# A two-layer decoder trunk in one kernel: MLP products in runs of one width, convolution tiles behind the next chunk's whole projection

## The chip, the cores and the metric

The kernel runs on one core of a Trainium2 chip. It uses that core's engines: PE (matmul), DVE (vector), ACT (activation), POOL, and SP, which here only issues DMAs. The metric is the time of the whole program on the device in microseconds, as the median of several runs.

## The reference, cut to what matters

Input is `x`, 512 tokens of 1024 channels, and a memory of 256 tokens. There are two layers. Layer 0 mixes tokens with a gated recurrence and pooling, layer 1 with a convolution module. Each layer then has a cross-attention into the memory and a gated MLP. The change touches the convolution module and the MLP:

```python
def conformer_conv(x, norm, w1, b1, dw_w, dw_b, ln_g, ln_b, w2, b2):
    h = rms_norm(x, norm) @ w1 + b1
    h = jax.nn.glu(h, axis=-1)
    h = causal_dwconv(h, dw_w, dw_b)
    h = jax.nn.silu(layer_norm(h, ln_g, ln_b))
    return h @ w2 + b2

def conv_ffn(x, norm, w_up, dw_w, dw_b, w_down):
    h = rms_norm(x, norm) @ w_up
    g = causal_dwconv(h[..., :D_FF], dw_w, dw_b)
    u = h[..., D_FF:]
    return (jax.nn.gelu(g) * u) @ w_down

for layer in range(DEPTH):
    ...
    x = x + cross_attn(x, mem, xa_norm[layer], xa_mem_norm[layer], xa_wq[layer], ...)
    x = x + conv_ffn(x, f_norm[layer], f_w_up[layer], f_dw_w[layer], ...)
return rms_norm(x, final_norm)
```

The convolution of the module has 31 taps per channel, `D_FF` is 3072.

## The kernel before

Channels lie on the 128 partitions and the 512 tokens along a row, so an activation is 8 chunks of 128 x 512. Every float32 operand of a large matmul is split into a high and a low part: ACT rounds the high part (a copy to the type fp32r), and DVE or POOL subtracts it from the operand (`split`, line 622). A full product then takes three matmuls, high x high, high x low and low x high (`mm3`, line 629).

**Who sets the order.** The program is written down first and ordered afterwards. Each call on an engine becomes a node of a recorder (`Recorder`, line 201) with a duration from `cost` (line 271). `plan` (line 319) plays the nodes through on a model of the engines. PE takes them nearly in the order of the code (a window of 60 nodes), the others by due time. Calls inside `rec.atomic()` are one node and are not torn apart. The order that comes out is fixed for each engine, and so is each tile's buffer. All planned instructions are issued in one line, 498, so the profile shows L498 for nearly everything and the tiles tell operations apart: `mm` and `aux` are PSUM accumulators (5 and 2 of them), `stat` one for statistics, `wf` raw weights, `wr` split weights (18 slots for both), `act` and `actf` activations, `h` the gated product in the conformer and the padded gate branch in the MLP, `tmp` short-lived.

**The MLP** (`ffn`, line 978) has 24 chunks of up-projection in each layer, in 6 groups of 4, and after each group's ups the previous group's down-projection, woven in. An up chunk (`up`, line 1006) is a 2 x 2 block scheme with seven products in place of eight (`product`, line 1012). Each product multiplies four row blocks. `b` holds the high parts of 256 columns and the low parts of the same 256 side by side, so one matmul of the high weights with all 512 columns and one of the low weights with the 256 high ones make a product of the block. From chunk 3 on (`PLAIN`, `both` in the code) the 512-wide form is used: for each j, first the 512-wide one, then the 256-wide one. In the first three chunks of a layer all matmuls have 256 columns. `copy` (line 1023) takes the running accumulator `x` to SBUF three times on the way.

**The conformer** (`conformer`, line 1331) has for each of its 8 chunks two projections of 24 matmuls with 512 columns. The first, the gate, goes through ACT's sigmoid (`gate`, line 1336). The second is multiplied with it by DVE (`gated`, line 1348), and four DMAs on SP then stack the result: each takes 32 channels and lays them out four times, shifted by one token each (`window(4)`). The convolution is shared. PE does 8 of the 31 taps with 32-wide tiles on the stacked copies into an `aux` accumulator (`conv_pe`, line 1370, two groups of four tiles; the last chunk has eight groups and so all its taps on PE). POOL and ACT do 4 taps (N_POOL), DVE does the other 19 by adding into the same accumulator (`conv`, line 1387). DVE's `merge` (line 1407) puts both together and so frees the accumulator; after chunk 3 and chunk 7 PE adds up channel sums for the layer norm (`quarters`, line 743). `pieces` (line 1341) loads and splits the weights of a chunk ahead of time. Behind the last convolution, while the layer norm goes through PE, DVE and ACT, PE has the value projections of the second layer's attention (`mem.values`, from weights loaded by `mem.piece`), and its last key projections (`mem.keys`). Before, the code of the loop reads: gate projection of c + 1, `conv_pe(c)`, second projection of c + 1, `conv(c)`.

Of the kernel before, what the change touches and what calls it, by code (L numbers as in the profile page):

```python
# [38 lines left out]
LAG = 5  # L39
PLAIN = 3  # L40
# [160 lines left out]
class Recorder:  # L201
# [69 lines left out]
    def cost(self, node, eng, method, args, how, reads):  # L271
        out = args[0]
        n = int(np.prod((reads[0] if not isinstance(out, View) else out).shape[1:]))
        if method == "dma_start":
            src = out if isinstance(out, View) else reads[0]
            node.tail += self.WIRE * 4 * n * src.shape[0] * (1.9 if "accum_op" in how else 1)
            window = any(k[0] == "window" for k in src.steps) or any(k[0] == "window" for r in reads for k in r.steps)
            node.us += 0.65 if window else {"SP": 0.42, "ACT": 0.42, "POOL": 0.6}[eng]
            return
        if eng == "PE":  # L280
# [3 lines left out]
            elif out.shape[0] == 32:  # L284
                node.us += 0.875 / 4
# [224 lines left out]
def trunk(ctx: ExitStack, tc: tile.TileContext, I: dict, out_t: bass.AP, out: bass.AP):  # L510
# [467 lines left out]
    def ffn(layer, norm, nxt):  # L978
# [27 lines left out]
        def up(c):  # L1006
# [5 lines left out]
            def product(ps, a, f, first, last):  # L1012
                wh, wl = w[a]
                for j in range(4):
                    q, b = slice(j * P, (j + 1) * P), norm.x[f, j]
                    first_j, last_j = first and j == 0, last and j == 3
                    with rec.atomic():
                        PE.matmul(ps, wh[:, q], b[:, :n], start=first_j, stop=False, skip_group_check=True)
                        if not both:
                            PE.matmul(ps, wh[:, q], b[:, H:], start=False, stop=False, skip_group_check=True)  # L1020
                        PE.matmul(ps[:, :H], wl[:, q], b[:, :H], start=False, stop=last_j, skip_group_check=True)
# [21 lines left out]
            product(x, "s2", N2, False, False)  # L1043
            s2 = copy(x)
            product(wps, "s4", B22, False, True)
            product(x, "s3", T3, False, False)
# [284 lines left out]
    def conformer(norm, nxt, mem, parked):  # L1331
# [98 lines left out]
        for c in range(C):  # L1430
            if c < C - 1:
                b = gate(c + 1, project(w[0], c + 1, norm.x))
                spread(c + 1)
            else:
                mem.keys(KE)
            conv_pe(c)
            if c < C - 1:
                gated(c + 1, b, project(w[1], c + 1, norm.x))
                if c < C - 2:
                    w = pieces(c + 2)  # L1440
            else:
                mem.eng = G
                ready = [mem.piece(i, park=True) for i in range(4)] + [mem.piece(i) for i in range(4, 8)]
            conv(c)
# [20 lines left out]
        for n in range(KE + 1, C):  # L1465
            mem.keys(n)
# [128 lines left out]
```

## Time and profile before

| | |
|---|---|
| median of 3 runs | 1436.5 us (1436.49 to 1437.42) |
| the profiled execution | 1437.59 us |
| its span in the trace | 1435.8 us |
| PE busy, share of the span | 99% |
| DVE busy, share of the span | 85% |
| ACT busy, share of the span | 59% |
| POOL busy, share of the span | 13% |
| mean granted clock of PE | 0.999 |

The durations below come from the one profiled execution, whose time is its span and 1.8 us around it. A row of a timeline gives the start from the beginning of the span, the length of the group, engine, line, operation, output and inputs, shape and count. Matmuls overlap: the length shown for one is longer than the distance to the next, so prices of matmuls are taken from the starts of groups that follow each other. A count of `128*32` tiles is twice that of the program, since the trace has each float32 matmul as two records.

### The profile page before, as it was taken

The page shows a single profiled execution, that of the slowest core. Times are in us where ns is not written, and L with a number is a line of the kernel's source. Part 1 is how long each engine was busy: PE and PEld are TensorE (multiplying, and loading weights), DVE is VectorE, ACT ScalarE, POOL GpSimd, SP SyncE. Part 2 cuts the span into 40 slices and gives each one's busy share as a digit, 9 for nine tenths or more (in the row PEclk, how much of TensorE's full clock was granted, in tenths as well). Part 3 has the DMA queues.
Part 4 walks back from the last instruction along what each step waited for, and adds up shares of the span by engine and source line. Part 5 has one row for each costly group of instructions (what it writes and reads, how often), then busy time and mean ns, then how long its engine had stood idle before and what let it go on. Part 6 is the DMA issues. An engine that isn't in the chain of part 4 may idle for free.

```text
span 1435.8 us, 20183 instructions
## 1 busy us (share of the span) xinstructions
PE 1425.5 (99%) x7512; PEld 1199.6 (84%) x7512; DVE 1223.2 (85%) x1874; ACT 850.8 (59%) x1298; POOL 185.2 (13%) x196
## 2 busy tenths in 40 slices
PE   9999999999999999999999999999999999999998
PEld 8888888888988888888886676888898888888888
DVE  8986964758999999999967996776699999999996
ACT  8578844446866656656643436644586665665654
POOL 0000000001110110110016663300111011111000
PEclk9999999999999999999999999999999999999999
DMA  9332322228877787876515472322688777777831
GB/s 346 106 103 74 125 94 90 77 88 224 234 206 208 193 222 184 222 199 178 174 57 140 132 230 74 117 88 82 176 219 216 200 215 205 207 213 183 209 93 60
DMA packets 75987, 231.91 MB, mean 162 GB/s; under 512 B 8560, under 2 KB 10608, under 8 KB 75888
## 3 DMA queue, kind: packets, MB, share of 16 engines
q1 hardware_dynamic: 61488, 192.20, 41.4%
q0 software_dynamic: 13824, 37.75, 15.1%
q8 instruction: 59, 0.97, 0.3%
q10 hardware_dynamic: 576, 0.67, 0.1%
q14 instruction: 40, 0.33, 0.1%
HBM read 207.52 MB, written 2.10 MB: 146 GB/s over the span
## 4 chain that ended last, share of the span: by engine, by line
PE 89%; DVE 7%; DMA 2%; issue 1%; ACT 1%; SPq 1%; DVEq 0%
PE mm L498 63%; PE aux L498 26%; DVE aux L498 3%; DVE wr L498 1%; DMA wf<-in_wv 1%; DVE act L498 1%; DVE tmp L498 1%; SPq L498 1%; DMA wf<-in_mem 1%; DMA actf<-h 0%; PE stat L498 0%; DVE actf L498 0%; DVE h L498 0%; DVE wf L498 0%; DVE x L498 0%
## 5 line engine op out<-in xcount | busy, mean ns | idle before, releaser
L498 PE MATMUL mm<-act,wr 128*128 128x512 f32 (+1 forms) x4599 | 990.8, 369 | 0.6 <-DVE act L498 0.6
L498 PEld LDWEIGHTS mm<-act,wr 128*128 128x128 f32 x4599 | 790.2, 188 | 151.6 <-issue 5.8
L498 ACT ACTIVATE wr<-wf 128x1024 fp32r<-128x1024 f32 x295 | 308.4, 1053 | 128.2 <-PE mm L498 45.2
L498 DVE TENSOR_TENSOR wr<-wf,wr 128x1024 fp32r<-128x1024 f32 x272 | 329.0, 1218 | 37.8 <-ACT wr L498 18.9
L498 PE MATMUL aux<-act,wr 128*128 128x256 f32 (+1 forms) x1509 | 294.4, 338 | 0.0
L498 PEld LDWEIGHTS aux<-act,wr 128*128 128x128 f32 x1509 | 235.5, 189 | 36.2 <-issue 0.5
L498 ACT ACTIVATE tmp<-aux 128x512 f32<-128x512 f32 (+1 forms) x189 | 108.0, 572 | 78.0 <-PE aux L498 76.7
L498 DVE TENSOR_TENSOR tmp<-tmp,tmp 128x512 f32<-128x512 f32 (+1 forms) x151 | 98.8, 656 | 13.5 <-ACT tmp L498 11.2
L498 ACT ACTIVATE act<-tmp 128x512 fp32r<-128x512 f32 (+1 forms) x85 | 52.9, 627 | 96.4 <-DVE tmp L498 96.3
L498 DVE TENSOR_TENSOR x<-x,mm 128x512 f32<-128x512 f32 (+1 forms) x126 | 81.4, 646 | 21.0 <-PE mm L498 20.2
L498 POOL DMA_DIRECT2D wf<-in_wup x48 | 41.9, 872 | 443.1 <-ACT act L498 272.6
L498 POOL DMA_DIRECT2D wf<-wf x48 | 41.3, 861 | 444.3 <-DMA wf<-in_wup 157.6
L498 DVE SCALAR_TENSOR_TENSOR aux<-h,par,aux 128x497 f32<-128x497 f32 (+18 forms) x133 | 93.2, 731 | 4.7 <-PE aux L498 2.1
L498 PE MATMUL aux<-act,act 128*128 128x512 f32 (+1 forms) x456 | 85.4, 330 | 0.3 <-ACT tmp L498 0.3
L498 ACT ACTIVATE act<-actf 128x512 fp32r<-128x512 f32 (+1 forms) x136 | 70.1, 535 | 25.9 <-DVE actf L498 23.9
L498 PEld LDWEIGHTS aux<-act,act 128*128 128x128 f32 x456 | 70.8, 189 | 10.9 <-ACT tmp L498 1.0
L498 DVE TENSOR_TENSOR act<-actf,act 128x512 fp32r<-128x512 f32 (+1 forms) x136 | 75.6, 582 | 2.2 <-ACT act L498 1.5
L498 DVE SCALAR_TENSOR_TENSOR tmp<-h,par,tmp 128x512 f32<-128x512 f32 x96 | 71.9, 749 | 1.8
L498 POOL TENSOR_TENSOR wr<-wf,wr 128x1024 fp32r<-128x1024 f32 x23 | 55.2, 2405 | 91.9 <-PE mm L498 35.8
L498 DVE TENSOR_TENSOR tmp<-mm,tmp 128x512 f32<-128x512 f32 x84 | 57.3, 684 | 10.0 <-PE mm L498 8.3
L498 ACT ACTIVATE tmp<-h,par 128x512 f32<-128x512 f32 (+3 forms) x69 | 52.5, 780 | 17.8 <-DVE h L498 17.1
L498 ACT ACTIVATE tmp<-mm 128x512 f32<-128x512 f32 (+1 forms) x58 | 33.2, 572 | 43.1 <-PE mm L498 43.0
(150 smaller groups left out, 1089.7 us busy)
## 6 DMA issues: line engine op xcount, KB each, us to landing
wf<-in_wup SPq DMA_DIRECT2D x144, 512.0 KB, 5.0
wf<-in_wup POOLq DMA_DIRECT2D x48, 512.0 KB, 6.7
wf<-in_wdown SPq DMA_DIRECT2D x48, 512.0 KB, 4.3
actf<-in_wup SPq DMA_DIRECT2D x48, 256.0 KB, 6.1
wf<-wf POOLq DMA_DIRECT2D x48, 256.0 KB, 6.0
wf<-in_pw SPq DMA_DIRECT2D x24, 512.0 KB, 3.9
wf<-in_win SPq DMA_DIRECT2D x20, 512.0 KB, 3.6
wf<-in_wk SPq DMA_DIRECT2D x16, 512.0 KB, 6.3
```

The source lines that it names most:

```text
L498: getattr(eng, method)(*[real(a) for a in args], **{k: real(v) for k, v in how.items()})
```

## The change

It has three parts.

1. `product` issues the four wide matmuls as one node and the four narrow ones as another. For the third accumulation into `x` and the one two products later (`s2` and `s3`, `flip`) the narrow ones come first, and neighbouring products then meet at the same width.
2. The conformer's loop counts half chunks. `AFTER = 2` puts a chunk's `conv_pe` and `conv` behind both projections of the next chunk; before, they stood around the second one. At the end two key projections (4 and 5) in place of one stand ahead of the last convolution, and two in place of three behind the value projections.
3. `cost` is told that a stacking copy occupies the wire twice as long and its issue takes 0.8 in place of 0.65, and that 32-wide matmuls cost a little more. These numbers only move instructions.

```diff
--- before
+++ after
 LAG = 5
+AFTER = 2
...
-            node.us += 0.65 if window else {"SP": 0.42, "ACT": 0.42, "POOL": 0.6}[eng]
+            node.tail *= 2.0 if window else 1.0
+            node.us += 0.8 if window else {"SP": 0.42, "ACT": 0.42, "POOL": 0.6}[eng]
...
             elif out.shape[0] == 32:
-                node.us += 0.875 / 4
+                node.us += 0.9 / 4 + (0.06 if how["start"] else 0.0)
...
-            def product(ps, a, f, first, last):
+            def product(ps, a, f, first, last, flip=False):
                 wh, wl = w[a]
-                for j in range(4):
-                    q, b = slice(j * P, (j + 1) * P), norm.x[f, j]
-                    first_j, last_j = first and j == 0, last and j == 3
+                b = [norm.x[f, j] for j in range(4)]
+                q = [slice(j * P, (j + 1) * P) for j in range(4)]
+
+                def high():
                     with rec.atomic():
-                        PE.matmul(ps, wh[:, q], b[:, :n], start=first_j, stop=False, skip_group_check=True)
-                        if not both:
-                            PE.matmul(ps, wh[:, q], b[:, H:], start=False, stop=False, skip_group_check=True)
-                        PE.matmul(ps[:, :H], wl[:, q], b[:, :H], start=False, stop=last_j, skip_group_check=True)
+                        for j in range(4):
+                            PE.matmul(ps, wh[:, q[j]], b[j][:, :n], start=first and j == 0, stop=last and flip and both and j == 3, skip_group_check=True)
+
+                def rest():
+                    with rec.atomic():
+                        for j in range(4):
+                            if not both:
+                                PE.matmul(ps, wh[:, q[j]], b[j][:, H:], start=False, stop=False, skip_group_check=True)
+                            PE.matmul(ps[:, :H], wl[:, q[j]], b[j][:, :H], start=False, stop=last and not (flip and both) and j == 3, skip_group_check=True)
+
+                for part in (rest, high) if flip and both else (high, rest):
+                    part()
...
-            product(x, "s2", N2, False, False)
+            product(x, "s2", N2, False, False, flip=True)
             s2 = copy(x)
             product(wps, "s4", B22, False, True)
-            product(x, "s3", T3, False, False)
+            product(x, "s3", T3, False, False, flip=True)
             s3 = copy(x)
...
-        for c in range(C):
-            if c < C - 1:
-                b = gate(c + 1, project(w[0], c + 1, norm.x))
-                spread(c + 1)
+        for i in range(2 * C - 2 + AFTER):
+            c = i // 2 + 1
+            if i >= 2 * C - 2:
+                mem.keys(KE + i - 2 * C + 2)
+            elif i % 2 == 0:
+                b = gate(c, project(w[0], c, norm.x))
+                spread(c)
             else:
-                mem.keys(KE)
-            conv_pe(c)
-            if c < C - 1:
-                gated(c + 1, b, project(w[1], c + 1, norm.x))
-                if c < C - 2:
-                    w = pieces(c + 2)
-            else:
+                gated(c, b, project(w[1], c, norm.x))
+                if c < C - 1:
+                    w = pieces(c + 1)
+            if i == 2 * C - 2:
                 mem.eng = G
-                ready = [mem.piece(i, park=True) for i in range(4)] + [mem.piece(i) for i in range(4, 8)]
-            conv(c)
+                ready = [mem.piece(k, park=True) for k in range(4)] + [mem.piece(k) for k in range(4, 8)]
+            c = i + 1 - AFTER
+            if c >= 0 and c % 2 == 0:
+                conv_pe(c // 2)
+                conv(c // 2)
...
-        for n in range(KE + 1, C):
+        for n in range(KE + AFTER, C):
             mem.keys(n)
```

PE's order in the first layer's MLP, the first product of an up chunk (`aux` is the running accumulator, the four `act` are the row blocks, `wr_4796` holds the high and `wr_4820` the low parts of the weights, in the second piece `wr_4673` and `wr_4711`), before:

```order
L498 MATMUL aux_4982<-act_3106,wr_4796 128x512
L498 MATMUL aux_4982<-act_3106,wr_4820 128x256
L498 MATMUL aux_4982<-act_3129,wr_4796 128x512
L498 MATMUL aux_4982<-act_3129,wr_4820 128x256
L498 MATMUL aux_4982<-act_3230,wr_4796 128x512
L498 MATMUL aux_4982<-act_3230,wr_4820 128x256
L498 MATMUL aux_4982<-act_3344,wr_4796 128x512
L498 MATMUL aux_4982<-act_3344,wr_4820 128x256
```

And after:

```order
L500 MATMUL aux_4836<-act_3114,wr_4673 128x512
L500 MATMUL aux_4836<-act_3121,wr_4673 128x512
L500 MATMUL aux_4836<-act_3232,wr_4673 128x512
L500 MATMUL aux_4836<-act_3329,wr_4673 128x512
L500 MATMUL aux_4836<-act_3114,wr_4711 128x256
L500 MATMUL aux_4836<-act_3121,wr_4711 128x256
L500 MATMUL aux_4836<-act_3232,wr_4711 128x256
L500 MATMUL aux_4836<-act_3329,wr_4711 128x256
```

The pairs of 512 and 256 columns became a run of each; the tiles and the count are the same.

PE's order in the conformer around the first chunk's convolution (`mm_7402` in the first piece is the second projection of chunk 1, `mm_7437` in the second piece the gate projection of chunk 2, `actf` the stacked copies, `aux` the convolution's accumulator), before:

```order
L498 MATMUL mm_7402<-act_7308,wr_7066 128x512
L498 MATMUL mm_7402<-act_7298,wr_7082 128x512
L498 MATMUL aux_7435<-actf_7370,wf_7075 32x512
L498 MATMUL aux_7435<-actf_7380,wf_7075 32x512
L498 MATMUL aux_7435<-actf_7387,wf_7075 32x512
L498 MATMUL aux_7435<-actf_7394,wf_7075 32x512
L498 MATMUL aux_7435<-actf_7370,wf_7075 32x508
L498 MATMUL aux_7435<-actf_7380,wf_7075 32x508
L498 MATMUL aux_7435<-actf_7387,wf_7075 32x508
L498 MATMUL aux_7435<-actf_7394,wf_7075 32x508
L498 MATMUL mm_7402<-act_7310,wr_7066 128x512
L498 MATMUL mm_7402<-act_7320,wr_7066 128x512
```

And after:

```order
L500 MATMUL mm_7437<-act_7298,wr_7099 128x512
L500 MATMUL mm_7437<-act_7286,wr_7116 128x512
L500 MATMUL aux_7478<-actf_7375,wf_7089 32x512
L500 MATMUL aux_7478<-actf_7383,wf_7089 32x512
L500 MATMUL aux_7478<-actf_7396,wf_7089 32x512
L500 MATMUL aux_7478<-actf_7402,wf_7089 32x512
L500 MATMUL aux_7478<-actf_7375,wf_7089 32x508
L500 MATMUL aux_7478<-actf_7383,wf_7089 32x508
L500 MATMUL aux_7478<-actf_7396,wf_7089 32x508
L500 MATMUL aux_7478<-actf_7402,wf_7089 32x508
L500 MATMUL mm_7437<-act_7300,wr_7099 128x512
L500 MATMUL mm_7437<-act_7310,wr_7099 128x512
```

Before, the tiles stand in the middle of chunk 1's second projection, 18 matmuls in; now that projection is whole, and they stand 15 matmuls into the gate projection of chunk 2, so 21 matmuls later.

DVE's order at the same place (`h_112` and `h_114` are the gated products of chunks 0 and 1, the rows on `aux` are chunk 0's taps, `wr<-tmp` the low parts of keys), before:

```order
L498 SCALAR_TENSOR_TENSOR h_112<-mm_7266,par,tmp_7348 128x512
L498 TENSOR_TENSOR wr_7413<-tmp_7152,wr_7400 128x256
L498 TENSOR_TENSOR wr_7413<-tmp_7177,wr_7400 128x256
L498 TENSOR_TENSOR wr_7413<-tmp_7215,wr_7400 128x256
L498 TENSOR_TENSOR wr_7413<-tmp_7327,wr_7400 128x256
L498 SCALAR_TENSOR_TENSOR aux_7435<-h_112,par,aux_7435 128x500
L498 SCALAR_TENSOR_TENSOR aux_7435<-h_112,par,aux_7435 128x499
L498 SCALAR_TENSOR_TENSOR aux_7435<-h_112,par,aux_7435 128x498
L498 SCALAR_TENSOR_TENSOR h_114<-mm_7402,par,tmp_7406 128x512
L498 SCALAR_TENSOR_TENSOR aux_7435<-h_112,par,aux_7435 128x497
```

And after:

```order
L500 SCALAR_TENSOR_TENSOR h_112<-mm_7268,par,tmp_7356 128x512
L500 SCALAR_TENSOR_TENSOR h_114<-mm_7398,par,tmp_7404 128x512
L500 TENSOR_TENSOR wr_7448<-tmp_7148,wr_7435 128x256
L500 TENSOR_TENSOR wr_7448<-tmp_7179,wr_7435 128x256
L500 TENSOR_TENSOR wr_7448<-tmp_7217,wr_7435 128x256
L500 TENSOR_TENSOR wr_7448<-tmp_7329,wr_7435 128x256
L500 SCALAR_TENSOR_TENSOR aux_7478<-h_112,par,aux_7478 128x500
L500 SCALAR_TENSOR_TENSOR aux_7478<-h_112,par,aux_7478 128x499
L500 SCALAR_TENSOR_TENSOR aux_7478<-h_112,par,aux_7478 128x498
```

The product of chunk 1 moved from behind the third tap to ahead of the first. Further on, taps of two chunks take turns more often: of the 133 taps between here and the last merge, 66 follow an instruction that wrote another tile, 60 before.

On SP two weight loads stand right ahead of the copies of chunk 2, where one stood; ahead of those of chunk 3 there are three, as before. The key piece 5 is loaded ahead of chunk 6's copies and split on POOL ahead of the value pieces. In the other MLP chunks, and in the second layer's MLP, the order changes as in the first place shown.

## The prediction

> **What bounds the kernel now.** I read the page's busy line first, then the windows view (span cut into stages; per engine the busy time and, in brackets, the instructions), then the waits, groups and timeline of the two stages that the change touches. In this order:
>
> ```profile
> PE 1425.5 (99%) x7512; PEld 1199.6 (84%) x7512; DVE 1223.2 (85%) x1874; ACT 850.8 (59%) x1298; POOL 185.2 (13%) x196
> 375.00:440.00 65.00, 64.63 (x379) 56.34 (x379) 63.91 (x99) 42.00 (x62) 8.07 (x10) 1.00 0.78 211
> 440.00:700.00 260.00, 260.00 (x1357) 221.37 (x1356) 247.34 (x361) 157.98 (x223) 25.66 (x30) 1.00 0.74 199
> 740.00:875.00 135.00, 132.87 (x671) 93.08 (x670) 115.18 (x170) 51.61 (x75) 75.64 (x54) 1.00 0.50 141
> PEld mm L498 <- ACT tmp L498: 0.2, 1, 0.2
> ```
>
> 375 to 740 is the first MLP; 440 to 700 is its steady part. There PE is busy for 260.00 of 260 us, its granted clock is 1.00, and the last row, all that the waits of PE's loads list in that stretch (PE's own list is empty), is a single 0.2 us. DVE has 247.34 of 260, 95%. So the MLP is bound by the rate at which PE streams matmuls, with DVE close behind: time taken off PE there is time off the span. 740 to 875 is the conformer, and it needs a closer look, since DVE's 115 of 135 is an average over two regimes. DVE's timeline there (start, duration, operation, count, and in brackets the idle time before it and what ended it):
>
> ```profile
> 759.33 2.08 DVE L498 TENSOR_TENSOR wr<-tmp,wr 128x256 fp32r<-128x256 f32 x3 [1.36 <-ACT wr L498]
> 763.34 2.30 DVE L498 SCALAR_TENSOR_TENSOR aux<-h,par,aux 128x500 f32<-128x500 f32 x3 [1.94 <-PE aux L498]
> 765.55 0.74 DVE L498 SCALAR_TENSOR_TENSOR h<-mm,par,tmp 128x512 f32<-128x512 f32 x1
> 766.21 13.66 DVE L498 SCALAR_TENSOR_TENSOR aux<-h,par,aux 128x497 f32<-128x497 f32 x18
> ...
> 791.86 3.07 DVE L498 SCALAR_TENSOR_TENSOR aux<-h,par,aux 128x500 f32<-128x500 f32 x4 [0.16 <-PE aux L498]
> ...
> 822.82 5.81 DVE L498 SCALAR_TENSOR_TENSOR aux<-h,par,aux 128x498 f32<-128x498 f32 x9
> 828.54 0.74 DVE L498 SCALAR_TENSOR_TENSOR actf<-aux,par,actf 128x512 f32<-128x512 f32 x1
> ...
> 844.15 0.74 DVE L498 SCALAR_TENSOR_TENSOR actf<-aux,par,actf 128x512 f32<-128x512 f32 x1
> ...
> 867.78 0.75 DVE L498 SCALAR_TENSOR_TENSOR actf<-aux,par,actf 128x512 f32<-128x512 f32 x1
> ```
>
> Taps are "aux<-h,par,aux", gated products "h<-mm,par,tmp", merges "actf<-aux". From the first tap at 763.34, which waited for PE's first convolution, to the last merge, over at 868.45 (867.78 and the 0.67 by which such rows follow each other, as 765.55 and 766.21), DVE stands idle once, for 0.16 us. That is a chain of 105.1 us whose start PE sets and whose pace DVE sets. PE's side of the same stretch:
>
> ```profile
> 740.82 20.57 PE L498 MATMUL mm<-act,wr 128*128 128x512 f32 x90
> 761.33 1.97 PE L498 MATMUL aux<-actf,wf 128*32 128x512 f32 x16
> 763.23 11.18 PE L498 MATMUL mm<-act,wr 128*128 128x512 f32 x48
> ...
> 786.03 1.05 PE L498 MATMUL aux<-actf,wf 128*32 128x512 f32 x4
> ...
> 789.92 1.90 PE L498 MATMUL aux<-actf,wf 128*32 128x512 f32 x10 [0.99 <-DMA actf<-h]
> 791.75 12.54 PE L498 MATMUL mm<-act,wr 128*128 128x512 f32 x54
> ...
> 817.21 2.91 PE L498 MATMUL aux<-actf,wf 128*32 128x512 f32 x16
> 820.04 9.81 PE L498 MATMUL mm<-act,wr 128*128 128x512 f32 x42
> ...
> 845.15 2.36 PE L498 MATMUL aux<-actf,wf 128*32 128x512 f32 x16
> 847.45 12.55 PE L498 MATMUL mm<-act,wr 128*128 128x512 f32 x54
> ...
> 872.72 1.06 PE L498 MATMUL stat<-actf,onesf 128*32 128x512 f32 x8
> ...
> 896.42 0.39 PE L498 MATMUL mm<-act,wr 128*128 128x512 f32 x1
> 897.42 2.93 PE L498 MATMUL mm<-act,wr 128*128 128x512 f32 x11 [0.60 <-DVE act L498]
> ```
>
> An undisturbed convolution ("aux<-actf,wf", 16 records) takes 1.90 us from its start to the next matmul (761.33 to 763.23). Chunk 2's takes 5.72 (786.03 to 791.75), because its stacked copies land late; chunk 4's takes 2.83 and chunk 6's 2.30. PE thus loses 3.8, 0.9 and 0.4, together 5.1 us. DVE felt 0.16 of it.
>
> **The MLP term.** The MLP has 24 chunks a layer; from the fourth on (21 x 2 layers = 42) each of its 7 products is four matmuls of 512 columns and four of 256, in turn before, in two runs after. The number of matmuls stays. The price of each width in a run of its own, from two stretches of PE's timeline, and what stands in the steady MLP, from the groups of 440 to 700 by form:
>
> ```profile
> 193.92 17.16 PE L498 MATMUL mm<-act,wr 128*128 128x512 f32 x75
> 210.92 0.84 PE L498 MATMUL aux<-act,wr 128*128 128x512 f32 x3
> 727.58 5.92 PE L498 MATMUL mm<-wr,act 128*128 128x256 f32 x48
> 733.33 0.95 PE L498 MATMUL stat<-onesf,tmp 128*128 128x1 f32 x8
> L498 PE MATMUL mm<-act,wr 128*128 128x512 f32 x609 | 172.6, 394 | 0.0
> L498 PE MATMUL aux<-act,wr 128*128 128x512 f32 x204 | 74.1, 398 | 0.0
> L498 PE MATMUL mm<-act,wr 128*128 128x256 f32 x204 | 57.3, 281 | 0.0
> L498 PE MATMUL aux<-act,wr 128*128 128x256 f32 x204 | 57.1, 280 | 0.0
> L498 PE MATMUL aux<-act,act 128*128 128x512 f32 x68 | 24.6, 396 | 0.0
> L498 PE MATMUL aux<-act,act 128*128 128x256 f32 x68 | 19.1, 280 | 0.0
> ```
>
> In runs, a 512 takes (210.92 - 193.92)/75 = 226.7 ns and a 256 takes (733.33 - 727.58)/48 = 119.8 ns. The stretch holds 609 + 204 + 68 = 881 of the one and 204 + 204 + 68 = 476 of the other: 881 x 0.2267 + 476 x 0.1198 = 199.7 + 57.0 = 256.7 us. It takes 260.0. Nothing waits, so the 3.3 us are the price of the turns: 3.3/476 = 6.8 ns for each pair. Before, a chunk has 7 x 4 = 28 changes from 512 to 256. After, products three to six stand as high-low, low-high, high-low, low-high, so neighbours share a width and 5 changes are left. Gain: 42 x 23 x 6.8 ns = **6.6 us**. With an error of 0.5 ns in the price of a 512 (0.44 us of the 3.3) the ends are 5.7 and 7.5; the trace has hardly a run of four of each width, so the price left on a change is taken to stay at 6.8.
>
> The Trainium skill ("TensorE: Matmul & The Clock Gate", section "Back-to-back issue gap") gives the spacing of lone warm matmuls as columns over 2.4 GHz plus about 2.5 ns, with no term for what stood before; by it this term would be zero. Its fixed part isn't this trace's either, where 226.7 ns for 512 columns leaves some 13.
>
> DVE must follow: its 247.3 us then stand in 260 - 3.3 x 23/28 = 257.3, or 96%. It fits, but in the first stretch DVE has 63.91 of 65, so some of the gain may wait for DVE there; the low end I take is half the gain, 3.3.
>
> **The conformer term.** The first convolution moves behind the first 15 matmuls of the next gate projection; in PE's order 21 matmuls more stand ahead of it, so it starts 21 x 0.2267 = 4.8 us later and DVE's first tap with it. On DVE's chain the gated product of chunk 1 goes ahead of the first tap, into idle time: -0.66. Taps that follow a tap of another chunk are cheaper: 9 of them in 828.54 - 822.82 = 5.72 us, 0.64 each, against 18 on one accumulator in 779.78 - 766.21 = 13.57 (the next product stands at 779.78), 0.75 each. DVE's order has 66 of the cheap ones now, 60 before: -0.7. The 0.16 goes. So the last merge ends at 868.45 + 4.8 - 0.7 - 0.7 - 0.2 = **871.7, 3.2 us later**.
>
> ```profile
> 779.78 0.74 DVE L498 SCALAR_TENSOR_TENSOR h<-mm,par,tmp 128x512 f32<-128x512 f32 x1
> ```
>
> The copies: chunk 2's product ended at 780.44 and its last copy released PE at 789.92, 9.5 us on. Now its projection is over before the convolution of chunk 1, the product ends near 778.6, the copies serve from 788.1, and PE, after 48 further matmuls (10.9 us), is there at 788.5. This wait goes. But an accumulator of the two is free for chunk 2 only when chunk 0 is merged, near 790.0 by the same DVE prices. The next wait is DVE's, and so for chunks 4 and 6 and the first sums: about 1.5, 1.9, 1.6 and 0.5 us, 5.5 in place of 5.1: what PE no longer waits for the copies it waits for DVE. Behind a waiting convolution the next gate projection is queued, and DVE's next product waits for that; but DVE reaches each product some 3 us after PE has it, so this costs nothing as long as the waits stay under that.
>
> With the key projections two further steps move: the fifth key piece's load comes ahead of chunk 6's copies on SP, and its split ahead of the value splits on POOL.
>
> ```profile
> L498 POOL TENSOR_TENSOR wr<-wf,wr 128x1024 fp32r<-128x1024 f32 x23 | 55.2, 2405 | 91.9 <-PE mm L498 35.8
> ```
>
> That is 2.4 us on POOL; the values start 3.4 us later on PE than before (after 848.1, a convolution of 1.9 and 18 narrow matmuls, 2.2, at 852.2, against 847.45 and six matmuls of 0.23, 848.8), so it stays covered; without that cover it would cost the 2.4. The planner's new numbers and the moved loads act through the orders alone.
>
> What counts is when the channel sums (872.72 now) and the layer norm behind them come. Chunk 4's merge ended at 844.81 and, shifted with the chain, ends at 848.0; then chunk 6's convolution can run. From there to the sums it was 872.72 - 845.15 = 27.6 us. In that place the order has 12 wide projection matmuls fewer (-2.7), 18 narrow key matmuls more (+2.2), no wait for the key weight or the copies (-0.9) and one convolution entry fewer (-0.3): 25.9. The sums stand at 873.9, **1.2 us later**. Between sums and the second projection PE holds 1.1 us less work, so it arrives at 896.4 as before, and waits for the layer norm, whose DVE chain is up to 1.4 us shorter, as two value scalings move into its gap: a loss between 1.2 and -0.2, taken at **0.5**. Bounds: the sums cannot precede the last merge, 871.8, so with the shorter chain the gain ends at 2.3; the whole delay carried through costs 4.8.
>
> Sum: -6.6 + 0.5 = -6.1. The profiled execution took 1437.6 (span 1435.8 and 1.8 around it), so 1431.5; it is 1.1 above the median of the runs, 1436.5, which becomes **1430.4**.
>
> **The rivals.** *The wait goes and nothing takes its place* (0.05): all 5.1 us come back, 1436.5 - 6.6 - 5.1 = 1424.8. Against it stands DVE's 0.16 us of idle time in 105. *DVE sets the MLP's pace* (0.08): half the gain, 1433.7; for it 63.91 of 65, against it the 12.7 us that DVE has free in 440 to 700. *Order does nothing* (0.08), as by the skill's rule: the 3.3 us would belong to the MLP's operands, MLP 0, 1437.0. For it: the trace has no long alternation outside the MLP. *Slower* (0.04): on SP's queue two weight loads now stand right ahead of chunk 2's copies, where there was one, and three ahead of chunk 3's. A row of before shows the queue held by such loads:
>
> ```profile
> 784.91 10.21 SPq L498 DMA_DIRECT2D wf<-in_pw  x3
> ```
>
> If each group waits 10.2 us for weight buffers with the copies behind it, a convolution slips 10.2, of which DVE's lead takes some 2.7; two places cost 15, so 1430.4 + 15 = 1445. It decides from 9 us of DVE idle time on. Against it: these are the three loads ahead of chunk 3's copies, as they stood before too, and DVE had its 0.16 us of idle time all the same.
>
> **How the numbers follow.** The forecast has the remaining 0.75. 1427.0 to 1434.5 holds its bounds (-7.5 and -2.3 reach 1426.7, -5.7 and +4.8 reach 1435.6; both ends at once are unlikely) and the DVE rival, 0.83. A measurement of this kernel can tell 0.2%, 2.9 us, from no change. Faster by more: the forecast 0.75, the first rival 0.05, half of the DVE rival, which lies on that line, 0.04: 0.84; within: its other half and the third rival, 0.12; slower 0.04.
>
> **What would show it.** Right: in the steady MLP, 260 us of the same work in some 257.3, with no new PE wait; conformer waits of PE on copies gone, waits on DVE's accumulators instead; first tap some 5 us later after the start of the gate projection, DVE without idle time to the last merge. Wrong: the same 260 us; PE waiting for DVE in the MLP; DVE idle between taps; or the sums no later than before with the projection following sooner.

## The result, and the profile after

The changed kernel takes 1434.84 us (median of 21 runs, 1434.42 to 1435.34), the kernel before 1436.95 us beside it (21 runs, 1436.45 to 1438.65): a ratio of 0.9985, 95% interval 0.9979 to 0.9991. It is 2.1 us faster where 6.1 were forecast, and lies just outside the range. The two profiled executions differ by 2.4 us of span (1435.8 and 1433.4). By the starts of matmuls in the two traces:

| stretch | before | after | |
|---|---|---|---|
| start to the first product of the first MLP | 356.49 | 356.26 | -0.23 |
| first MLP, to the statistics behind it | 376.84 | 374.91 | -1.93 |
| from there to the first product of the second MLP (conformer, attention) | 321.37 | 322.62 | +1.25 |
| second MLP, to the last matmul | 374.97 | 373.57 | -1.40 |

The busy line of the page after, the windows of the MLP's steady part and of the conformer, and what the waits view lists for PE and its loads in 440 to 700:

```profile
PE 1419.1 (99%) x7512; PEld 1198.6 (84%) x7512; DVE 1219.9 (85%) x1874; ACT 852.2 (59%) x1298; POOL 186.0 (13%) x196
440.00:700.00 260.00, 259.47 (x1360) 222.10 (x1359) 250.05 (x364) 160.31 (x227) 26.04 (x30) 1.00 0.74 200
740.00:875.00 135.00, 129.61 (x677) 92.65 (x676) 111.82 (x168) 51.26 (x74) 75.75 (x53) 1.00 0.52 145
PEld mm L500 <- ACT tmp L500: 1.9, 4, 0.9
PE mm L500 <- ACT tmp L500: 0.5, 1, 0.5
```

The steady MLP holds 1360 matmuls in 260 us where it held 1357, so some 0.7 us of work more (three of 512 columns), and not the 2.7 forecast. PE no longer stands at 260.00: it waits for ACT, 1.9 us at its loads where it was 0.2. In the conformer, PE's timeline and then DVE's:

```profile
763.92 1.92 PE L500 MATMUL aux<-actf,wf 128*32 128x512 f32 x16
...
788.21 1.92 PE L500 MATMUL aux<-actf,wf 128*32 128x512 f32 x16 [1.63 <-DVE actf L500]
...
818.80 1.92 PE L500 MATMUL aux<-actf,wf 128*32 128x512 f32 x16 [1.86 <-issue]
...
846.11 1.92 PE L500 MATMUL aux<-actf,wf 128*32 128x512 f32 x16 [1.61 <-issue]
...
872.36 1.06 PE L500 MATMUL stat<-actf,onesf 128*32 128x512 f32 x8
...
895.25 1.39 PE L500 MATMUL mm<-act,wr 128*128 128x512 f32 x4 [0.24 <-DVE act L500]
897.04 0.50 PE L500 MATMUL mm<-act,wr 128*128 128x512 f32 x1 [0.41 <-DVE wr L500]
```

```profile
765.91 10.01 DVE L500 SCALAR_TENSOR_TENSOR aux<-h,par,aux 128x500 f32<-128x500 f32 x13 [3.12 <-PE aux L500]
...
787.21 0.74 DVE L500 SCALAR_TENSOR_TENSOR actf<-aux,par,actf 128x512 f32<-128x512 f32 x1
...
817.95 0.74 DVE L500 SCALAR_TENSOR_TENSOR actf<-aux,par,actf 128x512 f32<-128x512 f32 x1
...
845.26 0.75 DVE L500 SCALAR_TENSOR_TENSOR actf<-aux,par,actf 128x512 f32<-128x512 f32 x1
...
868.70 0.75 DVE L500 SCALAR_TENSOR_TENSOR actf<-aux,par,actf 128x512 f32<-128x512 f32 x1
```

No convolution is stretched by its copies any more; ahead of chunks 2, 4 and 6 PE waits 1.63, 1.86 and 1.61 us for an accumulator, and each of these waits ends 0.1 to 0.3 us after the end of one of the first three merges in DVE's rows. DVE has no idle time from the first of these rows to the last. So the conformer went the way that was forecast. In the MLP the gain is half of what was forecast, and PE has new waits.

### The profile page after: what moved, and what is told of

It is laid out like the page before. It is cut to its first block, busy times and chain, and to the rows that moved or that the text cites. A ratio compares the mean times of both kernels' runs of the same rounds, so it can differ in the third digit from the quotient of the medians.

```text
span 1433.4 us, 20247 instructions
## 1 busy us (share of the span) xinstructions
PE 1419.1 (99%) x7512; PEld 1198.6 (84%) x7512; DVE 1219.9 (85%) x1874; ACT 852.2 (59%) x1298; POOL 186.0 (13%) x196
## 5 line engine op out<-in xcount | busy, mean ns | idle before, releaser
L500 PEld LDWEIGHTS mm<-act,wr 128*128 128x128 f32 x4599 | 801.7, 188 | 157.1 <-issue 5.8
L500 PE MATMUL aux<-act,wr 128*128 128x512 f32 (+1 forms) x1509 | 294.1, 337 | 0.3 <-DVE wr L500 0.2
L500 DVE SCALAR_TENSOR_TENSOR aux<-h,par,aux 128x499 f32<-128x499 f32 (+18 forms) x133 | 92.4, 730 | 5.5 <-PE aux L500 3.1
L500 PE MATMUL aux<-act,act 128*128 128x256 f32 (+1 forms) x456 | 84.4, 328 | 0.0
L500 PEld LDWEIGHTS aux<-act,act 128*128 128x128 f32 x456 | 73.7, 189 | 11.4 <-ACT tmp L500 0.5
L500 DVE TENSOR_TENSOR act<-tmp,act 128x512 fp32r<-128x512 f32 (+1 forms) x85 | 57.6, 681 | 0.4 <-ACT act L500 0.2
```

The costliest lines, as they stand in the source:

```text
L500: getattr(eng, method)(*[real(a) for a in args], **{k: real(v) for k, v in how.items()})
```

## The experiments

All times are compared with the kernel before in the same session (1436.8 to 1437.1 us). Three questions: what a change of width costs, where PE's new waits for ACT come from, and what sets the conformer.

### The two parts alone

`mlp_alone` is the kernel before with the new `product` and its two `flip=True`; `conf_alone` is the changed kernel with the old `product`.

> The kernel before with the new product alone; the conformer's order and the planner's numbers stay. Theory A, dearer edges: most of the price stays, because it sits on the wide matmuls that follow a step from 256 to 512 columns (about 15 ns for each such step that is left, 5 of 28 a chunk, where the turns cost about 6 each), and PE gets new waits for ACT's copy of the fifth product (about 2 us): 2.5 to 4 us faster than before, near 0.9977, and 440 to 700 us holds some 1.5 us of the gain at most. The prediction's price, 6.8 ns for each of 23 changes: 6.6 us faster, 0.9954. Theory B, DVE's pace: PE would wait for DVE in the MLP; A has waits for ACT alone.

> The kernel before with the conformer's new loop and the planner's new numbers alone; the products in the MLP stay in turns. Theory A, a loss behind the sums: 0.8 to 1.8 us slower than before, near 1.0009, with the first matmul of the second projection as early as before and the loss in waits inside it. The prediction's sum: 0.5 us slower, 1.0003. If the conformer's change were worth a gain that the MLP's change hides, it would be 1 us or more faster, 0.9993 or less.

Measured: 1433.2 us, 0.9972 (0.9961 to 0.9983), and 1438.34 us, 1.0008 (0.9999 to 1.0016). The MLP's part alone is worth 3.9 us, not 6.6. The conformer's part costs some 1.2 us; its interval just takes in no change, but the traces agree: the stretch between the MLPs takes 322.66 us with it, as in the changed kernel, and 321.11 with the MLP's part alone. The two parts add up to -2.7 us, where the changed kernel has -2.1.

### What a step from 256 to 512 columns costs

> Leaves out the whole computation and runs series of 64 long and 64 short matmuls on the same operands: long ones alone and short ones alone (512, 256, 384 and 128 columns), then 512 and 256 in turns and in runs of 2, 4, 8, 16 and 32, and 512 with 384 and 128 in turns and runs of 4. Theory A, dearer edges: 64 x (226.7 + 119.8) ns = 22.18 us is the price without a change; in turns about 0.4 us more (6 ns for each of 64 steps), in runs of 4 about 0.24 more (15 ns for each of 16), in runs of 8 0.12, of 16 0.06, of 32 0.03. The prediction's price, 6.8 ns for each: 0.44, 0.11, 0.05, 0.03 and 0.01 more. Tiles or operands: all series of 512 and 256 take the same.

Starts of the series in PE's timeline (each has 64 long and 64 short matmuls; `flat` only ends the last one):

```profile
39.87 0.39 PE L62 MATMUL long<-b,wh 128*128 128x512 f32 x1
...
68.88 0.28 PE L62 MATMUL short<-b,wh 128*128 128x256 f32 x1
...
84.24 0.40 PE L62 MATMUL one<-b,wh 128*128 128x512 f32 x1
...
106.85 0.64 PE L62 MATMUL two<-b,wh 128*128 128x512 f32 x2
...
129.16 0.63 PE L62 MATMUL four<-b,wh 128*128 128x512 f32 x2
...
151.61 0.63 PE L62 MATMUL eight<-b,wh 128*128 128x512 f32 x2
...
196.22 0.63 PE L62 MATMUL thirtytwo<-b,wh 128*128 128x512 f32 x2
...
218.45 0.34 PE L62 MATMUL flat<-b,wh 128*128 128x384 f32 x1
```

128 long ones take 68.88 - 39.87 = 29.01 us (226.6 ns each) and 128 short ones 15.36 (120.0), so 64 and 64 without a step are 22.19. In turns they take 22.61, in runs of two 22.31, of four 22.45, of 32 22.23. Per step from 256 to 512 that is 6.6 ns in turns (64 steps), 3.9 in runs of two (32), 17 in runs of four (16) and some 20 in runs of 32 (two steps). In the runs of eight the five wide matmuls behind a step stand 233, 236, 228, 232 and 231 ns apart before the spacing is 226.7 again, the first two narrow ones 113 and 119: 27 ns lost and 8 won back. In turns a single wide matmul stands behind each step, at 233, 241 or 236 ns in a cycle, with the narrow ones at 117, 120 or 113. **A step has no price of its own: it depends on how many wide matmuls follow**, and the prediction's 6.8 ns was the price in turns.

> Leaves out the whole computation and repeats the series of 64 and 64 in turns, in runs of 2 and in runs of 4, each once behind 16 matmuls of 512, of 256 and of 128 columns on another accumulator. In the first series the turns cost 6.7 ns a step, and nothing when they were run again at the end behind 128-column ones. Theory A, the run behind a step sets its price: 0.43, 0.13 and 0.27 us over 22.18 in all three places. Rival, the phase that the matmuls ahead leave sets it: the turns take 22.61 us behind two of them and 22.2 behind the 128-column ones, and runs of 2 and 4 may differ too.

The turns behind 512-column matmuls, and behind 128-column ones (each second row starts the next series):

```profile
43.41 0.39 PE L47 MATMUL longone<-b,wh 128*128 128x512 f32 x1
...
66.01 0.40 PE L47 MATMUL leadlongtwo<-b,wh 128*128 128x512 f32 x1
...
192.87 0.44 PE L47 MATMUL thinone<-b,wh 128*128 128x512 f32 x1
...
215.11 0.22 PE L47 MATMUL leadthintwo<-b,wh 128*128 128x128 f32 x1
```

22.60 and 22.24 us: the same turns cost 6.5 ns a step behind the one and 0.9 behind the other, all 64 of them. Runs of two took 22.29, 22.30 and 22.35, runs of four 22.43 and 22.45. So for turns the rival came true: they have two rhythms, and here what stood ahead set which. Runs of two and of four keep their price. In the MLP of the kernel before the turns go at the dear rhythm, as the table below shows.

In the kernel itself, first the flip taken back (`, flip=True)` removed twice), then runs of two (no flip):

```diff
-                for part in (rest, high) if flip and both else (high, rest):
-                    part()
+                for h in (0, 2):
+                    with rec.atomic():
+                        for j in (h, h + 1):
+                            PE.matmul(ps, wh[:, q[j]], b[j][:, :n], ...)
+                        for j in (h, h + 1):
...
+                            PE.matmul(ps[:, :H], wl[:, q[j]], b[j][:, :H], ...)
```

> The changed kernel with the narrow matmuls last in every product, so that a chunk has 7 steps from 256 to 512 columns in place of 5. Theory A, dearer edges (about 15 ns each): 42 x 2 x 15 = 1.3 us slower than the changed kernel, so about 0.9994 of the kernel before. The prediction's price, 6.8 ns each: 0.6 us slower, about 0.9989. If the price belongs to tiles or operands and not to the order: the same as the changed kernel, 0.9985. One thing more could move it: the last matmuls ahead of ACT's copies of the third and fifth accumulations are then narrow ones again, as in the kernel before, so the running accumulator's waits may change by some tenths of a microsecond.

> The changed kernel with each product in runs of two (two matmuls of 512 columns, two of 256, twice) and no flip: 14 steps from 256 to 512 columns in a chunk in place of 5. Theory A, the price of a step depends on the run behind it (19 ns where four or more of 512 columns follow, 3.9 ns in runs of two, as in the series): 14 x 3.9 = 55 ns a chunk in place of 5 x 19.4 = 97, so 42 x 42 ns = 1.8 us faster than the changed kernel, about 0.9973 of the kernel before, if the waits for ACT's copies stay. One price for every step: by 19.4 ns 7.3 us slower than the changed kernel (1.0036), by the prediction's 6.8 ns 2.6 us slower (1.0003).

Measured: 1437.44 us, 1.0002 (0.9993 to 1.0011), so 2.4 us slower than the changed kernel; and 1432.4 us, 0.9968 (0.9956 to 0.9981), 2.4 faster by the ratios. Counted over all 512- and 256-column matmuls of both MLPs, from the first product of each to the ends in the first table (the spacing of starts less 226.7 and 120.0 ns; a spacing over 250 or 140 ns is counted as a wait):

| kernel | steps | over the bare price, us | waits in it, us | per step, ns |
|---|---|---|---|---|
| before | 1180 | 11.6 | 3.2 | 7.1 |
| changed | 210 | 8.5 | 4.8 | 17.9 |
| MLP's part alone | 210 | 8.7 | 5.0 | 17.4 |
| no flip | 296 | 10.8 | 5.4 | 18.4 |
| runs of two | 594 | 5.8 | 3.8 | 3.3 |
| longer lead (below) | 218 | 7.5 | 3.8 | 17.1 |

The last column is what is left without the waits, for each step. An error of 0.1 ns in the 226.7 would move it by 1 ns in runs of four. A price of 17 to 18 ns for each step in runs of four holds over four kernels, 3.3 in runs of two, 7.1 in turns, close to the series (17, 3.9 and 6.6). Without the flip 86 steps more cost 1.7 us, and waits 0.6: 2.3 of the 2.4 measured.

### PE's new waits for ACT

`s4` can start on `wps` only when ACT has copied `wps` (`s5`). In `cover`, `product(wps, "s1", ...)` and its copy stand ahead of `product(yps, "a12", ...)`.

> The changed kernel with the product s1 and the copy of its result ahead of the product a12, so that ACT has two products and not one (2.8 in place of 1.4 us) between the end of s1 and the first matmul of s4, which needs the copy. Theory A, the new waits come from this short lead: PE's waits for ACT in both MLPs fall from some 4 us to some 2, and the time by 1.5 to 2 us, to about 0.9973 of the kernel before. Rival, ACT is late because of what is queued ahead of the copy, however early the product ends: the wait moves to another product's matmul and the time stays at 0.9985.

Measured: 1432.96 us, 0.9974 (0.9964 to 0.9983), 1.6 us below the changed kernel by the ratios, whose intervals overlap. In the traces 1.0 us of it stands in the two MLPs, as the counted waits in the table (3.8 in place of 4.8), and 0.5 ahead of the first MLP, where the code is the same. So the longer lead gave the MLPs 1.0 us where 1.5 to 2 were expected. The waits on ACT in 1073 to 1400 us, of the changed kernel and then of this one:

```profile
PEld mm L500 <- ACT tmp L500: 2.6, 6, 0.9
```

```profile
PEld aux L500 <- ACT tmp L500: 0.9, 3, 0.4
```

The waits of `mm` are gone from the list, and some on the running accumulator took their place. Why there are more of them since the change, ACT's timeline of the changed kernel shows, with PE's row behind it:

```profile
523.22 0.62 ACT L500 ACTIVATE act<-actf 128x512 fp32r<-128x512 f32 x1
524.13 1.06 ACT L500 ACTIVATE wr<-wf 128x1024 fp32r<-128x1024 f32 x1 [0.29 <-DVE wr L500]
525.09 0.61 ACT L500 ACTIVATE act<-actf 128x512 fp32r<-128x512 f32 x1
525.61 0.58 ACT L500 ACTIVATE tmp<-mm 128x512 f32<-128x512 f32 x1
...
526.24 1.67 PE L500 MATMUL mm<-act,wr 128*128 128x512 f32 x8 [0.47 <-ACT tmp L500]
```

and of the kernel before at the same copy:

```profile
526.01 0.60 ACT L498 ACTIVATE tmp<-mm 128x512 f32<-128x512 f32 x1 [1.31 <-PE mm L498]
```

Before, ACT waited 1.31 us for PE and then copied at once. Now the planner, for which PE's nodes changed, has put weight and activation splits ahead of the copy in ACT's fixed order; the copy starts when they are done, and PE waits. That the order does it is shown here for one place; the other places were not gone through.

### What sets the conformer

`old_numbers` takes the planner's three new numbers back, `new_numbers` keeps them with `AFTER = 1`, and `pool_five` has `N_POOL = [5] * 7 + [0]`.

> The changed kernel with the planner's numbers for copies and 32-wide matmuls as before; the loop stays (a convolution behind the next chunk's whole projection). The first convolution then stands 6 matmuls later than in the kernel before and not 21, and convolutions stand 48 matmuls apart. Theory A, the conformer's loss comes from DVE's chain starting 4.8 us late: the chain starts 1.4 us late, PE's waits for accumulators (1.6, 1.9 and 1.6 us) fall below 1 us each, and the time is 1 to 3 us below that of the changed kernel, 0.9965 to 0.9978. Rival, the copies: their waits (3.8, 0.9 and 0.4 us) come back and the time is that of the old conformer, about 0.9975, with waits on copies in the trace. Rival, the start does not matter: 0.9985.

> The changed kernel with the half-chunk count at 1 in place of 2, so that a convolution stands around the second projection as before, and with the planner's new numbers. In PE's order the first convolution stands 15 matmuls later than in the kernel before, so these numbers alone move most of it. Theory A, the numbers and not the loop cost the time: about 0.9982 to 0.9988, first tap 3.4 us later after the start of the stage than before. Rival, the loop costs it: about 0.9975, as with the product alone (0.9972).

> The changed kernel with five taps in place of four of each of the first seven chunks on POOL and ACT, so seven taps fewer on DVE; the first convolution stands at the same place in PE's order. DVE's order has 41 taps behind a tap of another chunk in place of 65, so its chain gets 7 x 0.7 = 4.9 us shorter by the taps and 24 x 0.11 = 2.6 us longer by the order, 2.3 us in all. Theory A, DVE's chain sets the conformer once it has begun: the last merge ends 2.3 us sooner after the end of the MLP (136 in place of 138.2 us), PE's waits for accumulators shrink, and the time is 1 to 2.5 us below the changed kernel, 0.9968 to 0.9978. Rival, PE's own work and the planner's order set it: 0.9985 or more, with the waits in other places.

Measured: 1436.32 us, 0.9995 (0.9987 to 1.0004); 1437.58 us, 1.0006 (0.9997 to 1.0015); 1438.66 us, 1.0011 (1.0002 to 1.0020). All three are 1.4 us or more slower than the changed kernel by the ratios, and no run of theirs is as fast as its slowest (1435.34). So **my theory of them falls**: an earlier first tap, or a chain of DVE that ends sooner, does not bring the time back. From the statistics behind the first MLP, in us:

| kernel | first tap | last merge over | channel sums | idle times in PE's timeline | whole stretch | stretch less waits |
|---|---|---|---|---|---|---|
| before | 30.0 | 135.1 | 139.4 | | 321.4 | |
| changed | 34.7 | 138.2 | 141.2 | 6.2 | 322.6 | 316.4 |
| old_numbers | 31.8 | 137.6 | 141.9 | 6.4 | 324.4 | 318.0 |
| new_numbers | 33.4 | 139.1 | 144.1 | 8.7 | 325.1 | 316.4 |
| pool_five | 34.7 | 137.3 | 144.2 | 7.9 | 327.6 | 319.7 |

(The first row's waits lie inside convolutions and can't be listed the same way.) The work of PE is the same, so what counts is how long PE waits in all, wherever it does, for accumulators, for key weights that DVE splits between taps, and for the layer norm. Two kernels lose more than they wait. Chunk 4's convolution with the clock of the 4 us that begin with it: of `old_numbers`, of `pool_five` and of the changed kernel:

```profile
816.70 3.01 PE L499 MATMUL aux<-actf,wf 128*32 128x512 f32 x16 [3.94 <-issue]
816.70:820.70 4.00, 4.00 (x19) 1.44 (x20) 3.86 (x6) 0.00 (x0) 4.00 (x3) 0.58 0.00 0
```

```profile
818.38 3.63 PE L500 MATMUL aux<-actf,wf 128*32 128x512 f32 x16 [4.35 <-issue]
818.40:822.40 4.00, 4.00 (x17) 1.09 (x18) 3.59 (x6) 1.27 (x3) 1.51 (x2) 0.50 0.01 3
```

```profile
818.80:822.80 4.00, 4.00 (x25) 2.26 (x26) 3.89 (x6) 0.48 (x1) 2.83 (x2) 1.00 0.00 0
```

A wait of 1.86 us left the granted clock at 1.00; behind 3.94 and 4.35 us it was 0.58 and 0.50 in the 4 us that follow, and the convolution took 3.0 and 3.6 us in place of 1.9.

> Leaves out the whole computation and runs series of 64 matmuls of 512 columns, between which PE waits for one to eight operations on DVE and a copy on ACT, so for some 1.5 to 6 us. In the run with five taps on POOL a convolution behind a wait of 4.35 us took 3.6 us in place of 1.9, at a granted clock of 0.50. Theory A, a wait above some length lowers the clock: series behind waits up to some 2.5 us take 64 x 0.2267 = 14.5 us, series behind waits of 4 us and more some 2 us longer, with a granted clock of 0.5 at their start. Rival, something else slowed that convolution: all series take the same.

Four of its pauses, the first matmul with its wait and the 63 behind it:

```profile
39.75 0.50 PE L38 MATMUL two<-r,wh 128*128 128x512 f32 x1 [1.91 <-ACT r L46]
40.09 14.46 PE L38 MATMUL two<-b,wh 128*128 128x512 f32 x63
...
56.91 0.80 PE L38 MATMUL three<-r,wh 128*128 128x512 f32 x1 [2.37 <-ACT r L46]
57.51 15.78 PE L38 MATMUL three<-b,wh 128*128 128x512 f32 x63
...
95.84 0.50 PE L38 MATMUL five<-r,wh 128*128 128x512 f32 x1 [3.29 <-ACT r L46]
96.18 14.48 PE L38 MATMUL five<-b,wh 128*128 128x512 f32 x63
...
114.41 0.50 PE L38 MATMUL six<-r,wh 128*128 128x512 f32 x1 [3.75 <-ACT r L46]
114.75 16.06 PE L38 MATMUL six<-b,wh 128*128 128x512 f32 x63
```

From the first start to the last end it is 14.8 us behind waits of 1.91 and 3.29 us (and of 1.45), and 16.4 behind 2.37 and 3.75 (16.3 to 16.4 behind 2.83, 4.21 and 4.68): 1.6 us more. That is what `old_numbers` (one wait of 3.94) has above 316.4, and twice that, for 4.35 and 2.83, what `pool_five` has. The Trainium skill ("TensorE: Matmul & The Clock Gate", section "HAM oscillation — how this bites in real kernels") puts the limit at gaps of about 3.4 us. Here 2.37 was enough once and 3.29 was not, while 2.18 in `new_numbers` left the granted clock at 1.00; so by these runs no wait over 2.3 us is safe. The changed kernel's waits all lie below.

The last open piece was what the changed kernel loses inside the last projection, where PE waits for DVE: its first 72 matmuls there take 18.36 us (894.61 to 912.97), before 17.45 (896.42 to 913.87), so 0.9 more. `pw2_on_pool` changes `load_w(I["pw2"][n])` to `load_w(I["pw2"][n], G)` for the first three weights.

> The changed kernel with the low parts of the first three weights of the conformer's last projection subtracted on POOL in place of DVE (2.4 us each there, 1.2 on DVE); everything ahead of the layer norm keeps its order. Theory C, what is left of the conformer's loss sits in that projection, where PE waits for DVE, which has these three splits between the steps of the layer norm: the time from the first matmul of the projection to the end of the stage shrinks, the stage takes 321.4 to 322.0 us in place of 322.6, and the time is 0.9977 to 0.9981. Rival, the weights come later from POOL and PE waits for them: 0.9985 or more.

Measured: 1437.0 us, 0.9999 (0.9990 to 1.0008), 2.0 us slower than the changed kernel; the stretch takes 324.9 us. The second and third of POOL's splits, DVE's subtractions beside them and behind them, PE's wait and its clock:

```profile
894.10 2.37 POOL L500 TENSOR_TENSOR wr<-wf,wr 128x1024 fp32r<-128x1024 f32 x1
896.42 2.85 POOL L500 TENSOR_TENSOR wr<-wf,wr 128x1024 fp32r<-128x1024 f32 x1
895.60 1.42 DVE L500 TENSOR_TENSOR act<-actf,act 128x512 fp32r<-128x512 f32 x1
896.94 2.87 DVE L500 TENSOR_TENSOR act<-actf,act 128x512 fp32r<-128x512 f32 x1
899.73 1.88 DVE L500 TENSOR_TENSOR act<-actf,act 128x512 fp32r<-128x512 f32 x3
897.07 5.82 PE L500 MATMUL mm<-act,wr 128*128 128x512 f32 x17 [2.36 <-DVE act L500]
897.10:901.10 4.00, 4.00 (x10) 2.87 (x11) 4.00 (x4) 3.90 (x7) 2.16 (x1) 0.60 0.34 140
```

and the same operation of DVE in the changed kernel, with POOL idle:

```profile
898.04 1.89 DVE L500 TENSOR_TENSOR act<-actf,act 128x512 fp32r<-128x512 f32 x3
```

Three in a row without POOL take 1.88 or 1.89 us. The two that began while a split ran on POOL took 1.42 and 2.87 us, and each ended some 0.55 us after that split: 897.02 behind 896.47, 899.81 behind 899.27. PE waited 2.36 us for them, and its clock fell. So the run does not tell whether the splits on DVE are what costs the 0.9 us; that stays open.

### Versions that beat both

`pairs_old_conf` is the kernel before with runs of two; `old_conf_best` adds the longer lead, `best` also the three splits on POOL; `new_conf_best` is the changed kernel with runs of two and the lead.

> The kernel before with the MLP's products in runs of two (no flip) and s1 with its copy ahead of a12; the conformer as before. Theory A, the two MLP terms found so far add up: product alone 0.9972, runs of two 2.5 us and the longer lead 1.9 us below the changed kernel, so 1437 x 0.9972 - 2.5 - 1.9 = 1428.6 us, 0.9941; the stage from the end of the first MLP to the start of the second takes 321.1 us, as with the product alone. Rival, both save the same waits: only the larger of the two counts, 1430.5, 0.9955.

> The same products in the changed kernel, with the conformer's new loop and numbers. Theory A, the conformer's change costs its 1.5 us whatever the MLP does: 1430.1 us, 0.9952, and the stage between the MLPs takes 322.6 us. Rival, the conformer's loss depends on the MLP ahead of it: as fast as the old conformer, 0.9941.

> The kernel before with the products in runs of two and nothing else. The kernel with the longer lead as well took 1430.9 us (0.9958), where the two terms together should have given 1428.6. Theory A, runs of two are worth the same on either conformer (2.5 us below the product in runs of four): 1433.2 - 2.5 = 1430.7, 0.9956, so the longer lead adds nothing where the runs are of two. Rival, the lead still counts and runs of two gave less here: 1431.5 to 1432.5, 0.9963 to 0.9969.

> The kernel before with runs of two, the longer lead and the three splits on POOL. Theory C, PE's wait of 0.6 us for DVE in the last projection of the old conformer goes: 0.5 us below the 1430.9 of the same kernel without the move, 0.9954. Rival, POOL is later with them: 0.9958 or more.

Measured: runs of two on the old conformer 1430.7 us, 0.9956 (0.9943 to 0.9968); with the lead 1430.88, 0.9958 (0.9946 to 0.9971); with POOL's splits 1435.92, 0.9991 (0.9982 to 1.0000); on the new conformer 1432.77, 0.9970 (0.9959 to 0.9981). POOL's splits cost the same way as above: PE waits 3.66 us for DVE at the last projection, where it is 0.61 without the move, and the granted clock is 0.50 in the 4 us that follow.

```profile
897.08 3.59 PE L498 MATMUL mm<-act,wr 128*128 128x512 f32 x7 [3.66 <-DVE act L498]
```

The lead adds nothing to runs of two, as its rival said: there PE's loads wait 0.8 us a layer for that copy, not 2.2 to 2.6. The old conformer is 1.9 us better under the same MLP. The fastest kernel is the one before with runs of two and nothing else: 6.4 us below before, some 4 below the changed one.

## Why the prediction was wrong, point by point

- **The MLP term, -6.6 us: the step that failed is "the price left on a change is taken to stay at 6.8".** The turns' price was right (6.6 in the series, 7.1 in the kernel). The 210 steps that are left cost 17.9 ns each, since four or more wide matmuls follow them. By steps that is (11.6 - 3.2) - (8.5 - 4.8) = 4.7 us of gain in place of 6.6. The bounds of 5.7 and 7.5 came from the price of a 512 alone; the text said itself that the trace has hardly a run of four of each width, and then left that unknown out of the range. The low end of 3.3, taken for DVE's sake, was near what came, but by luck: the cause was another.
- **"With no new PE wait" failed as well**: 4.8 us of waits in place of 3.2 took 1.6 back. The prediction looked for the engine that is nearly full, DVE, and not at ACT's order around the copy that PE needs soonest. What is left is 3.1 us.
- **The conformer's steps held.** First tap +4.7 (said 4.8), last merge at 138.2 from the statistics (871.7 - 733.3 = 138.4 said), waits of 1.6, 1.9 and 1.6 for accumulators (said 1.5, 1.9 and 1.6; the fourth wait, 0.5 at the first sums, is not in the trace), sums +1.8 (said 1.2), PE at the last projection +0.35 (said 0). What failed is the size of the last step, the loss taken at 0.5: it is 1.25, because behind that arrival PE loses another 0.9 inside the projection, which the sum ended ahead of. That is at the upper end of the 1.2 to -0.2 given for this step, and far inside the outer bounds.
- **The rivals.** That order does nothing is refuted: the same operands took 22.23 to 22.61 us by order alone. The Trainium skill ("TensorE: Matmul & The Clock Gate", section "Back-to-back issue gap"), whose rule stood beside that rival, has no term for what stood before. DVE didn't set the MLP's pace: the longest waits of PE and its loads, up to 0.9 us, are on ACT, and those on DVE come to 0.3 us in a layer. The conformer's waits did not go for nothing, and no weight load on SP held the copies. Each had been given 0.08 or less; the case that came true, a forecast mechanism at half its size, had no chance of its own.

Sum: -3.1 and +1.25, with -0.2 ahead of the first MLP, is -2.1, the difference of the medians. The two spans differ by 0.3 us more: 0.2 is in the rows behind the second MLP's last product, which the count by steps leaves out, and 0.1 behind the last matmul.

## What to carry to other kernels

Measure the price of an order in runs of the length that it will have: an average over turns says nothing of the step that stays when turns become runs. Here groups of two and two were better than turns and than runs of four. Where a planner fixes all engines' orders, a change on one engine moves the others too: read the order of the engine that must answer soonest. A wait of PE costs its length while it is short, and in these runs up to 1.6 us more once the clock drops behind it, so two waits below 2.3 us are better than one of the same sum.

## What the runs showed of the hardware

- Behind a step from 256 to 512 columns about five matmuls of 512 are slower, by 27 ns together, and the first two of 256 behind the opposite step faster by 8. With 384 in place of 256, turns cost 13 ns a step (64 of each took 26.45 us in place of 25.60). Turns can settle in two rhythms, at 6.5 or below 1 ns a step, by what stood ahead. The cause was not looked for.
- Waits of PE of 2.36 us and more lowered its granted clock to about half for some 3 to 4 us (0.50 in the whole 4 us behind 4.35 us), with one exception at 3.29.
- DVE's 128 x 512 operations on two tensors in SBUF take 0.63 to 0.70 us. In the traces of before, of the changed kernel, of `pw2_on_pool` and of `best`, 15 of 1748 took longer, 0.88 to 2.87 us. Each of the 15 had begun while an operation ran on POOL, and each ended 0.54 to 0.55 us behind the end of that one: DVE's was held until POOL's was done.
